# Small constants loaded behind a GpSimd read of a modulation chunk, and two modulation units transposed together

## The chip, the cores and the metric

The kernel runs on one core of a Trainium2 chip. A core has TensorE (PE in the profile, with its weight loads shown apart as PEld), VectorE (DVE), ScalarE (ACT), GpSimd (POOL) and SyncE (SP), each with an instruction stream of its own that runs in order. DMAs are issued by an engine's stream and carried out by the core's 16 DMA engines. The metric is the device time of one launch in microseconds, lower is better.

## The reference, cut to what matters

Two layers of a transformer trunk over 256 context tokens and 256 latent tokens, 1024 channels, in float32. Each layer begins so:

```python
mod_lat = (silu_c @ w_ada[l] + b_ada[l])[:, None, :]        # six shifts, scales, gates of 1024
mod_ctx = silu_ctx @ w_ada[l] + b_ada[l]
h_c = modulate(rms_norm(x_ctx, g_attn[l]), csh1, csc1)      # h * (1 + scale) + shift
h   = modulate(rms_norm(x_lat, g_attn[l]), sh1, sc1)
p = h @ w_in                                                # gates | c_q 768 | c_kv 256 | k_r 32 | q, k, v
mq = (rms_norm(c_q, g_qa) @ w_uq)
kv = (rms_norm(c_kv, g_kva) @ w_ukv)
mk = rms_norm(concat([k_nope, rope(k_r)]), g_mk)            # gains g_mla_q, g_mla_k, g_na_q, g_na_k
```

Two attentions follow (one dense, one over a window of a 4 x 64 grid with a learned position bias), a gated merge, an output projection and a squared-ReLU MLP. The small constants of this case are the gains `g_mla_q`, `g_mla_k`, `g_na_q`, `g_na_k`, the rope table, the window mask, a reversal matrix `rev`, and the second layer's biases and norm gains.

## The kernel before

Activations lie as [128 channels, 8 chunks, 512 tokens]. A product in float32 is made of three matmuls of float32r parts: `mm3` (L101 to L103) multiplies the high and low halves. A weight comes by `wraw` (L118, a DMA on SP's queue) into one of five `raw` buffers; `wsplit` makes `whi` on ACT (L127) and `wlo` on DVE (L128).

The opening of layer 0: `x` and the context are loaded and transposed, and the modulation of layer 0 that the first norm needs is computed in units. `ada_unit` (L183) loads two pieces of `w_ada` into `spare` buffers, multiplies them with `silu` on PE in float32 (L191), copies the sums on ACT (L197), transposes them on PE (L202), and finishes on DVE (L204, L208, and for a scale `A1` at L176). Groups of chunks `(0, 1), (1, 1), (2, 2), (4, 2), (6, 2)` (first chunk, how many) take a scale unit on PSUM bank C and a shift unit on bank D each (`ada2`, L474). `norm_apply` then makes `u` (L298, DVE, needs the scale), `h` high (L301, ACT, needs the shift) and `h` low (L303, DVE). The main product of that loop is c_q: per chunk 18 matmuls of 512 columns into six PSUM banks.

`late_consts` (L357) loads the constants with 16 DMAs on GpSimd's queue and then prepares them on DVE (L372 to L377). It is called behind the loop, with `tc.issue_after(r0_ins.ins)`, which lets its instructions be issued as soon as the reciprocal root of the first norm (L162) has been.

Behind that loop come, in this order of the program: the store of `xT` (L497), the evacuation of c_q (`lat_evac`, L508 to L512), the product for c_kv and k_r (`ckv_load`, `ckv_evac`, L595 to L619: copies `ckt` L600, squares L602 and L603 on ACT, `kr` L604, transposes L613, `G` at L617 and L618), a part of the modulation on DVE as side work (`ada_side`, L231 and L233, advanced by `step`), and the products with `w_uq` (three groups of heads, each of two loads) and `w_ukv`.

The engines' orders are not written by hand: a scheduler orders the instructions by the program's order, their dependencies and its own estimate of when each is ready. An edit in one place can therefore move instructions elsewhere. SP's order is the same in both kernels.

Of the kernel before, what the change touches and what calls it, by code (L numbers as in the profile page):

```python
# [7 lines left out]
F32 = mybir.dt.float32  # L8
F32R = mybir.dt.float32r
AF = mybir.ActivationFunctionType  # L10
ALU = mybir.AluOpType
AX = mybir.AxisListType.X

D = 1024
KD = 8
DEPTH = 2
# [6 lines left out]
NOPE = 64  # L23
# [22 lines left out]
def trunk(ctx: ExitStack, tc, t):  # L46
    nc = tc.nc
    PSUM = bass.MemoryType.PSUM
    const = ctx.enter_context(tc.tile_pool(name="const", bufs=1))
# [7 lines left out]
    def ps(tag):  # L57
        return pp.tile([128, 512], F32, tag="ps" + tag, name="ps" + tag, bufs=BANKS[tag])
# [19 lines left out]
    def bc(ap2d):  # L78
        return bass.AP(tensor=ap2d.tensor, offset=ap2d.offset, ap=[[0, 128]] + list(ap2d.ap))
# [36 lines left out]
    def wraw(w, k0, kc, c0, cols, alt=None):  # L116
        raw = v3(alt() if alt else raw_tile(), kc, cols)
        nc.sync.dma_start(  # L118
            out=raw,
            in_=w[k0 * 128:(k0 + kc) * 128, c0:c0 + cols].rearrange("(k p) f -> p k f", p=128),  # L120
        )
        return raw
# [27 lines left out]
    def step(n=1):  # L150
        while n and side:
            if next(side[0], side) is side:
                side.pop(0)
            else:
                n -= 1

    def rsqrt(dst, src):
        n = 1
        for d in src.shape[1:]:
            n *= d  # L160
        e = mhalf[:, 0:1].to_broadcast([128, n])
        return nc.gpsimd.tensor_tensor(out=dst, in0=src, in1=e, op=ALU.pow)  # L162
# [4 lines left out]
    A1 = [const.tile([128, KD, 2], F32, name=f"A1_{l}") for l in range(DEPTH)]  # L167
# [3 lines left out]
    def mod_use(l, j, f, n, m, zs=(0, 1)):  # L171

        if j in (1, 4):
            go = 48 if j == 1 else 56
            A = (A1 if j == 1 else A2)[l]
            nc.vector.scalar_tensor_tensor(  # L176
                out=A[:, f:f + n, zs[0]:zs[-1] + 1], in0=m, scalar=1.0,
                in1=pT[:, l, go + f:go + f + n].unsqueeze(2).to_broadcast([128, n, len(zs)]),
                op0=ALU.add, op1=ALU.mult)
        if j == 2:  # L180
            nc.vector.tensor_scalar(out=G1[l][:, f:f + n, zs[0]:zs[-1] + 1], in0=m, scalar1=0.5, scalar2=None, op0=ALU.mult)

    def ada_unit(l, j, f, bank="C", alt=None, defer=False, n=2):  # L183

        c0 = j * 8 + f
        o = ps(bank)
        for r in range(2):
            raw = wraw(t["w_ada"][l], r * 4, 4, c0 * 128, n * 128, alt)
            for g in range(4):
                k = r * 4 + g  # L190
                nc.tensor.matmul(  # L191
                    o[32 * g:32 * g + 32, :n * 128], silu[:, k], raw[:, g],
                    start=(r == 0), stop=(r == 1),
                    tile_position=(0, 32 * g),
                )
        s = sp.tile([128, 256], F32, tag="ada", name="ada", bufs=2)
        nc.scalar.activation(out=s[:, :n * 128], in_=o[:, :n * 128], func=AF.Copy)  # L197

        def second():
            o2 = ps(bank)  # L200
            for b in range(n):
                nc.tensor.transpose(o2[:, b * 128:(b + 1) * 128], s[:, b * 128:(b + 1) * 128], ident)  # L202
            m = modT[l][:, c0:c0 + n, :]
            nc.vector.tensor_reduce(  # L204
                out=m, in_=o2[:, :n * 128].rearrange("p (b g z) -> p b z g", b=n, g=4)[:, :, 0:2, :],
                op=ALU.add, axis=AX,
            )
            nc.vector.tensor_tensor(  # L208
                out=m, in0=m, in1=pT[:, l, c0:c0 + n].unsqueeze(2).to_broadcast([128, n, 2]), op=ALU.add)
            mod_use(l, j, f, n, m)  # L210

        if not defer:
            return second()
        ada_late.append(second)
# [60 lines left out]
    def r_bcast(r, T, bank="D"):  # L275
        o = ps(bank)
        for i in range(T // 128):
            nc.tensor.matmul(o[:, i * 128:(i + 1) * 128], r[:, i:i + 1].to_broadcast([128, 128]), ident,
                             start=True, stop=True)
        return o  # L280
# [30 lines left out]
    def load_rows(l, eng):  # L311
        o = 0
        for src, n in ((t["b_ada"][l], 48), (t["g_attn"][l], 8), (t["g_mlp"][l], 8), (t["g_qa"][l], 6),
                       (t["g_kva"][l], 2)):
            eng.dma_start(out=prow[l][o:o + n, :], in_=src.rearrange("(r q) -> r q", q=128))
            o += n
# [6 lines left out]
    warm = const.tile([128, 1], F32, name="warm")  # L323
# [3 lines left out]
    pre_ctx = ExitStack()  # L327
    xpool = pre_ctx.enter_context(tc.tile_pool(name="pre", bufs=1))
    xT = xpool.tile([128, KD, TT], F32, name="xT")
    gcm2 = xpool.tile([NOPE, DEPTH], F32, name="gcm2")  # L330
    gcn2 = xpool.tile([128, DEPTH], F32, name="gcn2")
    xrow = act.tile([128, 4096], F32, tag="G", name="xrow", bufs=2).rearrange("p (i d) -> p i d", i=4)
    for i in range(4):
        src = t["ctx"] if i < 2 else t["x"]
# [16 lines left out]
    def block_sum():  # L351
        id4 = ident.rearrange("p (q i) -> p i q", q=4)
        nc.vector.tensor_reduce(out=m32[:, 0:32], in_=id4, op=ALU.add, axis=AX)
        nc.vector.tensor_copy(m32[:, 32:128].rearrange("p (q i) -> p q i", q=3),
                              m32[:, 0:32].unsqueeze(1).to_broadcast([128, 3, 32]))

    def late_consts():  # L357
        dma = nc.gpsimd.dma_start
        dma(out=gqr, in_=bc(t["g_mla_q"][:, NOPE:QK]))
        dma(out=gkr, in_=bc(t["g_mla_k"][:, NOPE:QK]))  # L360
        dma(out=ropec, in_=t["rope"])
        dma(out=gcm[0:NOPE, :], in_=t["g_mla_q"][:, 0:NOPE].rearrange("l d -> d l"))
        dma(out=gcm2, in_=t["g_mla_k"][:, 0:NOPE].rearrange("l d -> d l"))
        for z in (0, HD):
            dma(out=gcn[z:z + HD, :], in_=t["g_na_q"].rearrange("l d -> d l"))
            dma(out=gcn2[z:z + HD, :], in_=t["g_na_k"].rearrange("l d -> d l"))
        dma(out=rev, in_=t["rev"])
        dma(out=wmask, in_=t["wmask"])
        load_rows(1, nc.gpsimd)

        keep, v = tc.keep_in_program_order, nc.vector
        keep(v.memset(gcm[NOPE:QK, :], 1.0))  # L372
        keep(v.tensor_scalar(out=gqr, in0=gqr, scalar1=QSC, scalar2=None, op0=ALU.mult))
        keep(v.scalar_tensor_tensor(out=gcm[0:NOPE], in0=gcm[0:NOPE], scalar=QSC, in1=gcm2, op0=ALU.mult, op1=ALU.mult))
        keep(v.scalar_tensor_tensor(out=gcn, in0=gcn, scalar=NSC, in1=gcn2, op0=ALU.mult, op1=ALU.mult))
        for l in range(DEPTH):
            keep(v.tensor_tensor(out=ropeq[:, l].rearrange("p a b d -> p (a b) d"),  # L377
                                 in0=ropec.rearrange("p a b d -> p (a b) d"),
                                 in1=gqr[:, l, :].unsqueeze(1).to_broadcast([128, 4, RD]), op=ALU.mult))
# [14 lines left out]
    ss0 = const.tile([128, 4], F32, name="ss0")  # L394
# [2 lines left out]
        nc.scalar.activation(out=junk, in_=xrow[:, i], func=AF.Square, accum_out=ss0[:, i:i + 1])  # L397
    nc.vector.tensor_scalar(out=ss0, in0=ss0, scalar1=1.0 / D, scalar2=EPS, op0=ALU.mult, op1=ALU.add)
    r0 = sp.tile([128, 4], F32, tag="rt", name="rt", bufs=4)
    r0_ins = rsqrt(r0, ss0)  # L400
    R0p = r_bcast(r0, TT, "A")
    R0 = sp.tile([128, TT], F32, tag="acc", name="R0", bufs=2)
    nc.vector.tensor_copy(R0, R0p)
# [45 lines left out]
    def flush():  # L449
        while ada_late:  # L450
            ada_late.pop(0)()

    for l in range(DEPTH):
# [20 lines left out]
        def ada2(gi):  # L474
            if l == 0 and gi < len(groups):
                k, n = groups[gi]
                ada_unit(0, 1, k, "C", alt, n=n)
                ada_unit(0, 0, k, "D", alt, n=n)

        ada2(0)  # L480
        for gi, (k0, n) in enumerate(groups):
            ks = range(k0, k0 + n)
# [9 lines left out]
        if l == 0:  # L492
            fill += [(1, j, f) for j in (4,3,5) for f in range(0, 8, 2)]
        if l == 0:
            with tc.issue_after(r0_ins.ins):
                late_consts()
        nc.sync.dma_start(out=xT_d, in_=xT)  # L497
        pre_ctx.close()
# [141 lines left out]
        if l == 0:  # L640
            block_sum()
            side.append(ada_side(((0, 2, (0, 1)),), lambda z: [ap.tile([128, TT], F32, tag="P", name="ada", bufs=4)
                                                               for _ in range(2)]))
            step(2)


        qrs, krr, krz = hstat("qrs"), hstat("krr"), hstat("krz")
# [274 lines left out]
        for f in range(0, 8, 2):  # L922
# [4 lines left out]
            for j in range(2):  # L927
# [9 lines left out]
                for b in range(2):  # L937
                    nc.vector.scalar_tensor_tensor(out=g2[:, b], in0=g2[:, b], scalar=1.0, in1=zs[b],
                                                   op0=ALU.add, op1=ALU.mult)
# [160 lines left out]
```

## Time and profile before

| | |
|---|---|
| three runs | 1344.7, 1344.02, 1344.84 us (median 1344.7) |
| the profiled execution | 1344.34 us |
| its span, first to last instruction | 1342.6 us |
| mean granted TensorE clock | 0.992 |
| bytes read from HBM, written | 195.15 MB, 11.53 MB |

In the profile, a row of the timeline gives start, duration, engine, line, operation, tiles written and read, shapes, count, and in brackets the idle time of the engine just before and what ended it. "DMA x" behind an arrow is the landing of that load. A row of the view by stages gives the stretch, its length, the busy time and number of instructions of PE, PEld, DVE, ACT and POOL, then the granted clock of PE, the mean busy share of the 16 DMA engines, and GB/s. A row of the waits gives who waited for whom, the sum in us, how often, and the longest. Rows of queues give packets, MB, and the share of the 16 engines' time; q0 is GpSimd's queue, q1 that of SP and ACT.

### The profile page before, as it was taken

The numbers are of one execution on the slowest core, as the hardware profiler recorded it, in microseconds if no ns is written. First come the engines' busy times: TensorE is split into PE (matmuls) and PEld (weight loads), VectorE is DVE, ScalarE is ACT, GpSimd is POOL, SyncE is SP. The second block draws the span as 40 slices with busy tenths as digits, with TensorE's granted clock in tenths as the row PEclk, the third lists the DMA queues.
The fourth block names the chain that finished last, engine by engine and source line by source line (L and its number), as shares of the span: only waits on it lengthen the run. The fifth ranks groups of instructions, "written<-read, shape, count | busy, mean of one in ns | idle before, by whom it ended". The sixth has DMA issues, their size and how long they took to land.

```text
span 1342.6 us, 20389 instructions
## 1 busy us (share of the span) xinstructions
PE 1306.7 (97%) x7825; PEld 1098.5 (82%) x7825; DVE 863.4 (64%) x1462; ACT 586.5 (44%) x1061; POOL 275.8 (21%) x296
## 2 busy tenths in 40 slices
PE   6999999999999989999999999998999999999997
PEld 4698888976687868888888888898889789899896
DVE  4589377867885588887574334765854766755453
ACT  3455366445423344331423313564654544554442
POOL 3035403401005003210201100056040121221111
PEclk8999999999999999999999999999999999999999
DMA  9865411544477645465473344575134769656652
GB/s 277 285 151 165 151 32 32 157 113 85 93 261 235 202 144 165 150 187 173 133 212 96 101 125 150 167 191 150 32 87 97 121 216 273 170 163 189 189 187 94
DMA packets 245985, 208.01 MB, mean 155 GB/s; under 512 B 24496, under 2 KB 226992, under 8 KB 245504
## 3 DMA queue, kind: packets, MB, share of 16 engines
q1 hardware_dynamic: 235856, 190.16, 49.9%
q10 hardware_dynamic: 9520, 16.29, 3.4%
q8 instruction: 61, 1.00, 0.3%
q0 software_dynamic: 512, 0.27, 0.2%
q14 instruction: 36, 0.29, 0.1%
HBM read 195.15 MB, written 11.53 MB: 154 GB/s over the span
## 4 chain that ended last, share of the span: by engine, by line
PE 57%; issue 5%; DMA 2%; DVE 1%; POOL 1%; ACT 1%; SPq 0%; POOLq 0%; ACTq 0%; DVEq 0%
PE psA L103 8%; PE psA L102 8%; PE psA L101 8%; PE psB L101 5%; PE psB L102 5%; PE psB L103 5%; PE psC L101 4%; PE psC L103 4%; PE psC L102 4%; DMA bias<-in_rpb_dram 1%; PE psD L833 1%; PE psC L806 1%; DMA raw<-in_w_ff_dram 1%; PE psD L101 1%; PE psD L102 1%
## 5 line engine op out<-in xcount | busy, mean ns | idle before, releaser
L128 DVE TENSOR_TENSOR wlo<-raw,whi 128x1024 fp32r<-128x1024 f32 (+3 forms) x254 | 311.8, 1229 | 209.2 <-ACT whi L127 203.4
L127 ACT ACTIVATE whi<-raw 128x1024 fp32r<-128x1024 f32 (+3 forms) x254 | 261.1, 1029 | 376.2 <-PE psA L102 110.1
L233 DVE SCALAR_TENSOR_TENSOR ada<-raw,silu,ada 128x1024 f32<-128x1024 f32 (+1 forms) x105 | 123.7, 1211 | 19.4 <-DMA raw<-in_w_ada_dram 19.3
L102 PE MATMUL psA<-wlo,h 128*128 128x256 f32 (+2 forms) x416 | 123.5, 297 | 0.5 <-DVE wlo L128 0.5
L101 PE MATMUL psA<-whi,h 128*128 128x256 f32 (+2 forms) x416 | 123.2, 296 | 0.0
L103 PE MATMUL psA<-whi,h 128*128 128x256 f32 (+2 forms) x416 | 122.8, 296 | 0.0
L102 PE MATMUL psA<-h,whi 128*128 128x512 f32 (+1 forms) x312 | 110.0, 354 | 0.0
L103 PE MATMUL psA<-h,wlo 128*128 128x512 f32 (+1 forms) x312 | 109.5, 353 | 0.0
L101 PE MATMUL psA<-h,whi 128*128 128x512 f32 (+1 forms) x312 | 109.0, 358 | 0.1
L101 PEld LDWEIGHTS psA<-whi,h 128*128 128x128 f32 x416 | 79.7, 192 | 2.9 <-issue 0.8
L102 PEld LDWEIGHTS psA<-wlo,h 128*128 128x128 f32 x416 | 79.7, 192 | 2.4 <-DVE wlo L128 0.8
L103 PEld LDWEIGHTS psA<-whi,h 128*128 128x128 f32 x416 | 79.7, 192 | 1.9 <-issue 0.4
L983 POOL TENSOR_TENSOR fl<-s,fa 128x512 fp32r<-128x512 f32 (+1 forms) x32 | 38.3, 1198 | 176.6 <-ACT fa L982 176.6
L103 PE MATMUL psB<-h,wlo 128*128 128x512 f32 (+1 forms) x208 | 72.5, 349 | 0.0
L102 PE MATMUL psB<-h,whi 128*128 128x512 f32 (+1 forms) x208 | 72.5, 349 | 0.0
L101 PE MATMUL psB<-h,whi 128*128 128x512 f32 (+1 forms) x208 | 72.2, 350 | 0.0
L983 POOL TENSOR_TENSOR h<-s,h 128x512 fp32r<-128x512 f32 (+1 forms) x32 | 36.9, 1153 | 169.2 <-ACT h L982 169.2
L101 PEld LDWEIGHTS psA<-h,whi 128*128 128x128 f32 x312 | 58.3, 190 | 12.6 <-issue 6.3
L103 PEld LDWEIGHTS psA<-h,wlo 128*128 128x128 f32 x312 | 59.4, 190 | 10.0 <-issue 3.1
L767 POOL TENSOR_TENSOR bias<-bias,wmask 128x512 f32<-128x512 f32 x16 | 21.7, 1355 | 223.2 <-DMA bias<-in_rpb_dram 183.9
L102 PEld LDWEIGHTS psA<-h,whi 128*128 128x128 f32 x312 | 59.4, 190 | 9.8 <-issue 2.9
L101 PE MATMUL psA<-G,whi 128*128 128x512 f32 (+1 forms) x184 | 65.1, 354 | 0.0
(353 smaller groups left out, 3363.9 us busy)
## 6 DMA issues: line engine op xcount, KB each, us to landing
raw<-in_w_ff_dram SPq DMA_DIRECT2D x128, 512.0 KB, 4.2
raw<-in_w_ada_dram SPq DMA_DIRECT2D x62, 512.0 KB, 4.2
raw<-in_w_in_dram SPq DMA_DIRECT2D x56, 512.0 KB, 4.1
spare<-in_w_ada_dram SPq DMA_DIRECT2D x30, 512.0 KB, 7.2
raw<-in_w_out_dram SPq DMA_DIRECT2D x16, 512.0 KB, 6.3
raw<-in_w_in_dram SPq DMA_DIRECT2D x16, 384.0 KB, 5.4
xT_d<-xT SPq DMA_DIRECT2D x2, 2048.0 KB, 11.8
bias<-in_rpb_dram SPq DMA_DIRECT2D x64, 64.0 KB, 7.1
```

The costliest lines, as they stand in the source:

```text
L101: nc.tensor.matmul(out, sh, mh, start=first, stop=False)
L102: nc.tensor.matmul(out, sh, ml, start=False, stop=False)
L103: nc.tensor.matmul(out, sl, mh, start=False, stop=last)
L127: nc.scalar.activation(out=hi, in_=src, func=AF.Copy)
L128: nc.vector.tensor_tensor(out=lo, in0=src, in1=hi.bitcast(F32), op=ALU.subtract)
L233: nc.vector.scalar_tensor_tensor(out=a, in0=raw[:, c:c + w], scalar=sc, in1=a, op0=ALU.mult, op1=ALU.add)
L767: nc.gpsimd.tensor_tensor(out=bias.rearrange("p a i j -> p (a i) j"), in0=bias.rearrange("p a i j -> p (a i) j"), in1=wmask.unsqueeze(1).t ...
L806: nc.tensor.transpose(o[:, kt * 256 + i * 128:kt * 256 + (i + 1) * 128], pt[:, (kp * 2 + kt) * 128:(kp * 2 + kt + 1) * 128], perm if K == ...
L833: return nc.tensor.matmul(yo[z * 64:(z + 1) * 64, oc], vsel(kt, 2 * hp + z), tr[kt // 2][:, kt % 2, :], start=kt == 0, stop=kt == nkt - 1, ...
L983: nc.gpsimd.tensor_tensor(out=al[:, f, :], in0=s[:, :TQ], in1=ah[:, f, :].bitcast(F32), op=ALU.subtract)
```

## The change

Four edits. The DMAs of `late_consts` are issued behind a new GpSimd instruction that reads `A1` of layer 0, chunk 5, and writes a scratch value. The DVE part of `late_consts` becomes `late_gains`, called later, after the first two steps of the side work. The two helper tiles `gcm2` and `gcn2` move to a pool that lives on. And `ada2` defers both units' second halves (transposes, reduction, sums) until both units' matmuls and copies are written.

```diff
-    gcm2 = xpool.tile([NOPE, DEPTH], F32, name="gcm2")
-    gcn2 = xpool.tile([128, DEPTH], F32, name="gcn2")
+    gcm2 = const.tile([NOPE, DEPTH], F32, name="gcm2")
+    gcn2 = const.tile([128, DEPTH], F32, name="gcn2")
...
         load_rows(1, nc.gpsimd)
 
+    def late_gains():
+
         keep, v = tc.keep_in_program_order, nc.vector
         keep(v.memset(gcm[NOPE:QK, :], 1.0))
...
-    r0_ins = rsqrt(r0, ss0)
+    rsqrt(r0, ss0)
...
-                ada_unit(0, 1, k, "C", alt, n=n)
-                ada_unit(0, 0, k, "D", alt, n=n)
+                ada_unit(0, 1, k, "C", alt, True, n)
+                ada_unit(0, 0, k, "D", alt, True, n)
+                flush()
...
-            with tc.issue_after(r0_ins.ins):
+
+            gate = nc.gpsimd.tensor_scalar(out=warm, in0=A1[0][:, 5, 0:1], scalar1=0.0, scalar2=0.0,
+                                           op0=ALU.mult, op1=ALU.add)
+            with tc.issue_after(gate.ins):
                 late_consts()
...
             step(2)
+
+        if l == 0:
+            late_gains()
```

The orders of the engines show where that puts things. On POOL, in the opening, the change's order has the gate (L499, `A_0_100` is `A1` of layer 0) ahead of the first constant:

```order
L162 TENSOR_TENSOR rt<-ss_187,mhalf 128x4
L499 TENSOR_SCALAR warm<-A_0_100 128x1
L359 DMA gqr<-in_g_mla_q_dram 128x2x32
L360 DMA gkr<-in_g_mla_k_dram 128x2x32
L361 DMA ropec<-in_rope_dram 128x128
```

Before, the DMA of `gqr` followed L162 directly; nothing else moved on POOL.

On DVE, in the c_kv stage, before the change (L233 is the side work of the modulation, L128 the split of a `w_uq` tile where it is 864 wide, `psA` the second pair of token blocks):

```order
L233 SCALAR_TENSOR_TENSOR ada<-raw,silu,ada 128x512 x3
L604 TENSOR_TENSOR kr<-psD,gkr 128x32
L618 SCALAR_TENSOR_TENSOR G<-psC,pT,G 128x256
L128 TENSOR_TENSOR wlo<-raw,whi 128x864
L233 SCALAR_TENSOR_TENSOR ada<-raw,silu,ada 128x512
L618 SCALAR_TENSOR_TENSOR G<-psC,pT,G 128x256
L600 COPY ckt<-psA 128x256
L270 TENSOR_SCALAR ms<-psD 128x4
L128 TENSOR_TENSOR wlo<-raw,whi 128x864
L600 COPY ckt<-psA 128x256
L233 SCALAR_TENSOR_TENSOR ada<-raw,silu,ada 128x512
L604 TENSOR_TENSOR kr<-psA,gkr 128x32 x2
```

and with it (L606, L610 and L624 are the L600, L604 and L618 of before):

```order
L233 SCALAR_TENSOR_TENSOR ada<-raw,silu,ada 128x512
L374 MEMSET gcm 32x2
L375 TENSOR_SCALAR gqr<-gqr 128x64
L376 SCALAR_TENSOR_TENSOR gcm<-gcm,gcm_114 64x2
L377 SCALAR_TENSOR_TENSOR gcn<-gcn,gcn_115 128x2
L379 TENSOR_TENSOR ropeq<-ropec,gqr 128x128 x2
L128 TENSOR_TENSOR wlo<-raw,whi 128x864
L606 COPY ckt<-psA 128x256
L270 TENSOR_SCALAR ms<-psD 128x4
L606 COPY ckt<-psA 128x256
L128 TENSOR_TENSOR wlo<-raw,whi 128x864
L610 TENSOR_TENSOR kr<-psA,gkr 128x32 x2
```

The L233 that opens the second piece is the fourth; the fifth, which stood between the two L618 before, now stands behind the two `kr`. The six preparations of the constants, which stood some 30 rows earlier, stand ahead of the first 864-wide `wlo`.

On ACT, in the same stage, before the change:

```order
L127 ACTIVATE whi<-raw 128x864
L617 ACTIVATE G<-psC,pT 128x256
L127 ACTIVATE whi<-raw 128x864
L602 ACTIVATE sq,kvss<-psA 128x256
L603 ACTIVATE sq,krs<-psA 128x32
L602 ACTIVATE sq,kvss<-psA 128x256
L603 ACTIVATE sq,krs<-psA 128x32
L617 ACTIVATE G<-psC,pT 128x256 x2
L671 ACTIVATE mqk<-psA 128x288
```

and with it (L608, L609, L623 and L680 are the L602, L603, L617 and L671 of before):

```order
L623 ACTIVATE G<-psC,pT 128x256
L127 ACTIVATE whi<-raw 128x864
L608 ACTIVATE sq,kvss<-psA 128x256
L609 ACTIVATE sq,krs<-psA 128x32
L608 ACTIVATE sq,kvss<-psA 128x256
L609 ACTIVATE sq,krs<-psA 128x32
L127 ACTIVATE whi<-raw 128x864
L623 ACTIVATE G<-psC,pT 128x256 x2
L680 ACTIVATE mqk<-psA 128x288
```

The last 864-wide `whi` of each piece is that of the third `w_uq` tile: it stood ahead of the squares of the second pair of token blocks, and now stands behind them.

## Prediction

> **What bounds the kernel now.** I read the page's engine table first, then its slices, then who waited for whom on PE.
>
> ```profile
> span 1342.6 us, 20389 instructions
> PE 1306.7 (97%) x7825; PEld 1098.5 (82%) x7825; DVE 863.4 (64%) x1462; ACT 586.5 (44%) x1061; POOL 275.8 (21%) x296
> PE   6999999999999989999999999998999999999997
> ...
> PE psC L735 <- POOL mqk L701: 3.5, 1, 3.5
> PE psD L191 <- DMA spare<-in_w_ada_dram: 2.4, 1, 2.4
> PE psC L613 <- DVE ckt L600: 1.1, 1, 1.1
> PE psA L101 <- DVE kr L604: 0.7, 1, 0.7
> ```
>
> TensorE is the bound: 1306.7 of 1342.6 us. Only the first of the 40 slices falls well below 9. So a change can win only where PE waits. Three of the waits quoted lie in the first 130 us, which is all the program that this change reorders: 2.4 us for a modulation weight, 1.1 us for the copy `ckt`, 0.7 us for `kr`. The profiled execution took 1344.34 us, 1.74 us more than its span. My sum is made against it. The median of the three runs, 1344.7, is 0.36 us higher.
>
> **Part 1: the constants leave the opening.** Stages first (PE, PEld, DVE, ACT, POOL busy, then granted clock, DMA share, GB/s), then the queues inside 16 to 20 us and inside 20 to 32 us.
>
> ```profile
> 12.00:16.00 4.00, 4.00 (x36) 2.80 (x34) 2.65 (x5) 2.42 (x6) 2.65 (x4) 1.00 1.15 318
> 16.00:20.00 4.00, 2.89 (x50) 1.46 (x49) 3.31 (x11) 1.80 (x5) 4.00 (x8) 1.00 0.84 103
> 20.00:27.00 7.00, 4.73 (x18) 3.45 (x19) 3.73 (x10) 2.70 (x6) 3.90 (x8) 0.51 1.08 328
> 40.00:56.00 16.00, 16.00 (x110) 10.23 (x103) 9.38 (x26) 6.36 (x14) 0.00 (x0) 1.00 0.97 357
> ...
> q0 software_dynamic: 78, 0.11, 54.3%
> q1 hardware_dynamic: 607, 0.30, 30.1%
> ...
> q0 software_dynamic: 434, 0.16, 6.4%
> ```
>
> DMA delivers 318 GB/s, then 103, then 328. In the bad 4 us, GpSimd's queue q0 holds the engines 54.3% of the time for 0.11 MB, and the weights' queue q1 gets 30.1%. Without q0 the weights gain 0.543 x 4 = 2.2 us of all engines, up to (318-103)/318 x 4 = 2.7 us by bytes. The later constants hold 6.4% of 12 us, 0.8 us.
>
> ```profile
> 19.76 0.91 ACT L301 ACTIVATE h<-u,modT 128x256 fp32r<-128x256 f32 x2 [0.62 <-DVE modT L208]
> 22.27 0.65 PE L191 MATMUL psD<-spare,silu 128*32 128x128 f32 x8 [2.39 <-DMA spare<-in_w_ada_dram]
> 22.86 1.22 PE L101 MATMUL psA<-h,whi 128*128 128x512 f32 x2
> ```
>
> PE stands 2.39 us before L191, and behind it in PE's order stand the first main matmuls, at 22.86. The weight would land 2.2 to 2.7 us earlier. The next thing late is `h` of chunk 0, ready at 19.76 + 0.91 = 20.67, unchanged. The first main matmul can therefore start near 20.7, about 2.1 us earlier. Bounds: 0, if this load is late for another reason, and -2.7. I take **-2.1**, the row of `h`.
>
> **Part 2: the constants arrive later.** Their gate reads `A1` of chunk 5, written at 41.83 + 0.16.
>
> ```profile
> raw<-in_w_in_dram SPq DMA_DIRECT2D x8, 384.0 KB, 7.7
> ...
> 40.79 0.93 SPq L118 DMA_DIRECT2D raw<-in_w_in_dram  x2
> 41.77 0.50 SPq L497 DMA_DIRECT2D xT_d<-xT  x1
> 41.83 0.16 DVE L176 SCALAR_TENSOR_TENSOR A<-modT,pT 128x4 f32<-128x4 f32 x1
> 52.90 0.64 PE L191 MATMUL psD<-spare,silu 128*32 128x256 f32 x8
> 53.94 0.84 ACT L127 ACTIVATE whi<-raw 128x768 fp32r<-128x768 f32 x1
> 14.33 0.93 POOL L359 DMA_DIRECT2D gqr<-in_g_mla_q_dram  x1
> 26.15 0.51 POOL L315 DMA_DIRECT2D prow<-in_g_kva_dram  x1
> 77.11 0.18 DVE L604 TENSOR_TENSOR kr<-psC,gkr 128x32 f32<-128x32 f32 x1
> ```
>
> All 16 issues took 26.15 + 0.51 - 14.33 = 12.3 us, so they run from 42 to 55. Behind the gate on POOL stand only these DMAs, and then the bias additions after 76 us. The first reader is `kr` at 77.11, 22 us after the last issue. The burst now meets the load of chunks 6 and 7 (issued 40.79, used at 53.94) and the 2 MB store of `xT`, which PE does not wait for. It takes at most 2.7 us from the weights, and 53.94 - 41.72 is 12.2 us, against the 7.7 us that such loads of 384 KB take to land in the opening (median, first row). Cost 0. With that cover gone it would be 2.7.
>
> The Trainium skill, "DMA: Bandwidth & Descriptors", section "Issuing engines are not separate DMA queues", speaks against the change: DMAs of all issuing engines share the same 16 DMA engines and interleave. The rows of q0 and q1 agree (54.3% beside 30.1%). By that rule the burst costs its 2.2 us wherever it lands while DMA is full (0.97 in 40 to 56 us), and the sum would be 2.1 us worse; by the rows it takes the time from the store.
>
> **Part 3: the units' transposes together.** The counts of matmuls, copies and reductions are the same. Only the order changes: the scale unit's transposes now stand on PE behind the shift unit's matmuls, so `A1` comes later by a block of eight L191 at most, 0.64 us (row 52.90). What hides it: `h` needs the shift unit too, and its wait at 19.76 was ended by that unit's `modT` (L208), not by `A1`. If it were not hidden it would cost up to 0.6 once, since only the first group stands ahead of an idle PE; grouping the transposes could as well spare PE a change between kinds of matmul, of which no row gives a price by itself, so I bound the gain by the same block. Bounds -0.6 to +0.6, taken as 0.
>
> **Part 4: the late gains and what the scheduler moved with them.** This decides more than the diff suggests.
>
> ```profile
> 79.91 0.47 DVE L618 SCALAR_TENSOR_TENSOR G<-psC,pT,G 128x256 fp32r<-128x256 f32 x1
> 58.58 0.06 DVE L372 MEMSET gcm<- 32x2 f32 x1
> 58.92 0.48 DVE L377 TENSOR_TENSOR ropeq<-ropec,gqr 128x128 f32<-128x128 f32 x2
> 83.40 0.75 DVE L233 SCALAR_TENSOR_TENSOR ada<-raw,silu,ada 128x512 f32<-128x512 f32 x1 [2.05 <-DMA raw<-in_w_ada_dram]
> 84.94 0.45 PE L613 MATMUL psC<-ident,ckt 128*128 128x128 f32 x1 [1.15 <-DVE ckt L600]
> 87.50 0.93 ACT L127 ACTIVATE whi<-raw 128x864 fp32r<-128x864 f32 x1 [5.91 <-DMA raw<-in_w_uq_dram]
> 89.33 0.37 PE L101 MATMUL psA<-whi,G 128*128 128x288 f32 x1 [0.73 <-DVE kr L604]
> 82.00:85.00 3.00, 1.85 (x15) 1.62 (x15) 1.60 (x5) 0.00 (x0) 0.00 (x0) 1.00 0.79 194
> 85.00:88.40 3.40, 3.30 (x13) 2.85 (x13) 1.91 (x3) 0.90 (x2) 1.87 (x2) 0.50 0.78 250
> 88.40:89.30 0.90, 0.21 (x2) 0.00 (x0) 0.19 (x1) 0.90 (x9) 0.65 (x1) 0.99 0.38 155
> ```
>
> The six DVE instructions take 58.92 + 0.48 - 58.58 = 0.8 us. They leave an idle place and now stand ahead of `wlo`. But the fifth L233, which waited 2.05 us for its DMA ahead of both `ckt` copies, now stands behind them, and so does ACT's L127 of the third `w_uq` tile, which waited 5.91 us ahead of the squares that `kr` needs. Both PE waits lose their cause. PE lost 1.15 idle, 1.65 at half clock (half of 3.30) and 0.69, together 3.5 us; the later `wlo` gives back some 0.4, leaving 3.1.
>
> What is late next?
>
> ```profile
> 95.12 2.02 DVE L128 TENSOR_TENSOR wlo<-raw,whi 128x864 fp32r<-128x864 f32 x2
> 96.82 0.29 PE L102 MATMUL psA<-wlo,G 128*128 128x288 f32 x1
> 89.30:96.70 7.40, 7.37 (x56) 7.40 (x57) 7.16 (x13) 3.97 (x11) 6.96 (x11) 1.00 0.29 74
> 96.70:118.00 21.30, 21.30 (x163) 20.60 (x161) 20.02 (x34) 12.17 (x25) 6.25 (x9) 1.00 0.77 230
> ```
>
> The third `w_uq` tile. Its ACT split still waits for the same DMA, near 87.5, and the order puts the same twelve L233 ahead of its `wlo` as before, plus the 0.8 us of gains, which fall into the time in which DVE waited before. I put that `wlo` at 95.1 again: ready at 96.1, and PE used it at 96.82. DVE is busy 7.16 of 7.40 us there, so there is little to catch up with. PE's gain of 3.1 shrinks to 96.82 - 96.1 = **-0.7**, and PE stands idle some 2.4 us ahead of 96 instead. The row 85.00:88.40 shows what followed such a gap: 3.4 us at half clock, 1.7 us of work. Before, it lay partly beside waits; after 96.7 PE is busy without a gap. Bounds 0 and 1.7; I take **+1.2**, since DVE, 20.02 of 21.30 busy, hides part.
>
> Sum: -2.1 - 0.7 + 1.2 = -1.6 us. 1344.34 - 1.6 = **1342.7 us**, all else carried through, since PE is never long without work afterwards.
>
> **Rivals.**
> *Both gains stay* (0.22): the third tile's `wlo` comes 2.4 us earlier, because the two DVE waits vanish and their time is not refilled, and no clock is lost. 1344.34 - 2.1 - 3.1 = 1339.1. For it: DVE waited 2.05 us at 83.40. Against: 87.50, the same DMA.
> *The wait moves and grows* (0.10), the slower one: the third `w_uq` load needs the buffer that the eighth modulation product (the fourth L233) frees, and ahead of it now stand two L618 at 0.47 and one L604 at 0.18. It lands 1.1 us later, the gains' 0.8 us are not hidden, and the clock stays half for as long as from 20 to 27 us, 3.4 us lost: -2.1 + 1.9 + 3.4 = +3.2, 1347.5. With half as long a spell 1345.8. It decides from a `wlo` that starts more than 2.1 us later than 95.1, counted from the first main matmul, as the opening's gain is then used up. For it: 0.50 in the row of 85.00. Against: the load's landing at 87.5 was set by a DMA stage at 0.78, not by its issue.
> *The opening's gain fails or is paid back at 42 to 55 us* (0.13): -1.6 + 2.1, 1344.8; that the gate did not hold the loads back is in it, though POOL's order puts it first.
>
> The Trainium skill, "TensorE: Matmul & The Clock Gate", Part 1, says the clock is judged in free-running windows of about 3.4 us and is full again after one busy window. The 3.40 us row agrees, the 7 us one only as two windows. By the rule, the opening's half clock could end one window earlier and the sum would be about 0.6 us better.
>
> **How the numbers follow.** Forecast 0.55, with its own range 1341.2 to 1344.2. A measurement of this kernel tells about 0.2%, 2.7 us, from no change: 1342.0 to 1347.4 counts as same. Faster: the first rival and a fifth of the forecast, 0.33. Slower: half of the second rival, 0.05. Same 0.62. The range 1339.6 to 1346.2 leaves out half of the first rival and half of the second.
>
> **What would show it.** Right: GB/s in 16 to 20 us near 320; first L101 near 20.7; no wait of PE for `ckt` or `kr` before 95; a wait for `wlo` ahead of the second w_uq group. Wrong: the L191 wait still above 1 us; PE waiting between 40 and 56 us; no gap before that `wlo`, which would be the first rival.

## The result, and the profile after

The changed kernel takes **1338.96 us** (median of six runs, 1335.59 to 1340.72), the kernel before 1344.77 (six runs, 1341.44 to 1346.71). The ratio is 0.9948, with a 95% interval of 0.9931 to 0.9965: 5.8 us or 0.5% faster. The forecast was 1342.7, with a range down to 1339.6; the rival "both gains stay" had 1339.1. The profiled execution took 1338.82 us. A run far outside the others (3249.89 us in one of transposes_only, 1590.79 and 5351.93 in two of the kernel before) counts in no ratio below.

The page of the changed kernel, its engines and the slices of PE:

```profile
span 1337.0 us, 20381 instructions
PE 1305.0 (98%) x7825; PEld 1097.4 (82%) x7825; DVE 862.5 (65%) x1462; ACT 587.3 (44%) x1061; POOL 278.9 (21%) x297
PE   7999999999999989999999999998999999999997
```

PE's busy time fell by 1.7 us and the span by 5.6: most of what went is idle time. The same shows in who waited for whom on PE from 14 to 130 us:

```profile
PE psA L102 <- DVE wlo L128: 1.1, 1, 1.1
PE psA L101 <- ACT h L301: 0.8, 1, 0.8
```

The waits for L191's weight (2.4), for `ckt` (1.1) and for `kr` (0.7) are gone. Two new ones stand first: 0.8 us for `h`, and 1.1 us for a `wlo`. The stages (PE, PEld, DVE, ACT, POOL, then granted clock, DMA share, GB/s):

```profile
16.00:20.00 4.00, 3.31 (x55) 2.08 (x57) 3.23 (x9) 1.46 (x4) 0.00 (x0) 1.00 0.77 210
20.00:27.00 7.00, 6.22 (x35) 4.69 (x27) 4.29 (x14) 2.81 (x6) 0.00 (x0) 0.76 1.05 343
40.00:56.00 16.00, 16.00 (x100) 10.82 (x99) 10.80 (x26) 7.51 (x15) 9.51 (x16) 1.00 1.00 358
82.00:85.00 3.00, 3.00 (x25) 3.00 (x24) 1.12 (x4) 1.29 (x2) 2.61 (x2) 1.00 0.85 283
85.00:88.40 3.40, 3.40 (x27) 3.24 (x26) 3.40 (x7) 2.27 (x6) 3.23 (x7) 1.00 0.07 27
89.30:96.70 7.40, 6.25 (x47) 6.02 (x47) 7.40 (x12) 2.73 (x6) 3.64 (x6) 1.00 0.61 202
```

In 16 to 20 us DMA moves 210 GB/s where it moved 103. The granted clock of the opening is 0.76 over 20 to 27 us where it was 0.51. From 40 to 56 us the constants are loaded (16 instructions on POOL) and PE is busy 16.00 of 16.00. From 82 to 88.4 us PE is full at full clock, where it stood, and then ran at half clock, before.

To measure stages across kernels I use two marks. The c_kv stage begins about where DVE first evacuates c_q (L512 of the kernel before), and the first modulation's side work ends at L255. DVE's timeline, before:

```profile
66.56 0.75 DVE L512 SCALAR_TENSOR_TENSOR G<-psA,pT,G 128x512 fp32r<-128x512 f32 x1
127.27 0.72 DVE L255 TENSOR_TENSOR modT<-psC,pT 32x16 f32<-32x16 f32 x4
```

and after, where L512 has become L518, with the split of the third `w_uq` tile between them (the first of the two in that row):

```profile
63.91 0.75 DVE L518 SCALAR_TENSOR_TENSOR G<-psA,pT,G 128x512 fp32r<-128x512 f32 x1
90.80 2.03 DVE L128 TENSOR_TENSOR wlo<-raw,whi 128x864 fp32r<-128x864 f32 x2
122.45 0.72 DVE L255 TENSOR_TENSOR modT<-psC,pT 32x16 f32<-32x16 f32 x4
```

The opening is 66.56 - 63.91 = **2.65 us** shorter, and the stage between the marks lasts 58.54 us where it lasted 60.71, **2.17 us** less. The view by stages over just that stretch, before and after:

```profile
66.56:127.27 60.71, 58.47 (x394) 54.79 (x393) 54.19 (x98) 33.17 (x76) 25.91 (x38) 0.97 0.64 162
63.91:122.45 58.54, 57.15 (x394) 53.62 (x393) 54.48 (x105) 33.72 (x76) 27.03 (x38) 1.00 0.64 168
```

PE has the same 394 matmuls and is idle for 2.24 us before and 1.39 after. The clock is 0.97 before: one spell of 3.4 us at half clock (85.00 to 88.40), 1.7 us of work. After, there is none. From the second mark to the end the two profiles differ by another 0.8 us, which the last section explains.

### The profile page after: what moved, and what is told of

Same layout as the page of the kernel before. It is cut to its first block, busy times and chain, and to the rows that moved or that the text cites. A ratio compares the mean times of both kernels' runs of the same rounds, so it can differ in the third digit from the quotient of the medians.

```text
span 1337.0 us, 20381 instructions
## 1 busy us (share of the span) xinstructions
PE 1305.0 (98%) x7825; PEld 1097.4 (82%) x7825; DVE 862.5 (65%) x1462; ACT 587.3 (44%) x1061; POOL 278.9 (21%) x297
## 4 chain that ended last, share of the span: by engine, by line
PE 57%; issue 5%; DMA 2%; DVE 2%; ACT 2%; POOL 1%; SPq 0%; POOLq 0%; ACTq 0%; DVEq 0%
PE psA L101 8%; PE psA L103 8%; PE psA L102 8%; PE psB L101 5%; PE psB L102 5%; PE psB L103 5%; PE psC L101 4%; PE psC L102 4%; PE psC L103 4%; DMA bias<-in_rpb_dram 1%; PE psC L815 1%; DVE wlo L128 1%; PE psD L842 1%; PE psD L101 1%; PE psD L103 1%
## 5 line engine op out<-in xcount | busy, mean ns | idle before, releaser
L128 DVE TENSOR_TENSOR wlo<-raw,whi 128x1024 fp32r<-128x1024 f32 (+3 forms) x254 | 311.6, 1229 | 210.8 <-ACT whi L127 203.8
L233 DVE SCALAR_TENSOR_TENSOR ada<-raw,silu,ada 128x1024 f32<-128x1024 f32 (+1 forms) x105 | 121.9, 1196 | 18.2 <-DMA raw<-in_w_ada_dram 18.1
L101 PE MATMUL psA<-G,whi 128*128 128x512 f32 (+1 forms) x184 | 65.4, 355 | 0.0
L102 PE MATMUL psA<-G,whi 128*128 128x512 f32 (+1 forms) x184 | 65.3, 355 | 0.0
```

The lines of the kernel that those rows point to most:

```text
L101: nc.tensor.matmul(out, sh, mh, start=first, stop=False)
L102: nc.tensor.matmul(out, sh, ml, start=False, stop=False)
L128: nc.vector.tensor_tensor(out=lo, in0=src, in1=hi.bitcast(F32), op=ALU.subtract)
L233: nc.vector.scalar_tensor_tensor(out=a, in0=raw[:, c:c + w], scalar=sc, in1=a, op0=ALU.mult, op1=ALU.add)
```

## The experiments

All runs first, with the two marks of their profiles; after_again, after_third and gate_transposes_again repeat a kernel. A ratio is to the runs of the kernel before in the same job. "Order" says where ACT's split `whi` of the third `w_uq` tile stands: ahead of the squares of the last c_kv tokens, as before, or behind them, as after. "Opening" is the start of the row of L512, "stage" the time from there to L255.

| kernel | gate | transposes | gains | order | opening | stage | median (runs) | ratio to before, 95% |
|---|---|---|---|---|---|---|---|---|
| before | no | apart | old | ahead | 66.56 | 60.71 | 1344.77 (6) | |
| after | yes | together | late | behind | 63.91 | 58.54 | 1338.96 (6) | 0.9948 [0.9931, 0.9965] |
| after_again | yes | together | late | behind | 61.62 | 57.85 | 1338.39 (7) | 0.9962 [0.9945, 0.9979] |
| after_third | yes | together | late | behind | 62.34 | 58.06 | 1338.08 (7) | 0.9964 [0.9947, 0.9982] |
| gate_only | yes | apart | old | ahead | 64.31 | 60.37 | 1342.26 (10) | 0.9984 [0.9966, 1.0002] |
| transposes_only | no | together | old | behind | 65.88 | 58.10 | 1340.9 (7) | 0.9962 [0.994, 0.9983] |
| gains_only | no | apart | late | ahead | 66.98 | 62.09 | 1344.15 (10) | 1.0001 [0.9986, 1.0017] |
| gate_gains | yes | apart | late | ahead | 63.36 | 59.75 | 1340.94 (6) | 0.9965 [0.995, 0.998] |
| gate_transposes | yes | together | old | behind | 63.85 | 56.90 | 1336.69 (4) | 0.9938 [0.9915, 0.996] |
| gate_transposes_again | yes | together | old | behind | 62.79 | 57.17 | 1337.19 (8) | 0.9954 [0.9936, 0.9972] |
| act_order_only | no | apart | old | behind, forced | 64.96 | 58.64 | 1342.44 (10) | 0.9996 [0.9982, 1.0011] |
| gate_act_order | yes | apart | old | behind, forced | 62.81 | 58.20 | 1338.6 (10) | 0.9964 [0.995, 0.9979] |
| broadcasts_late | two loads | apart | old | ahead | 63.78 | 58.66 | 1341.28 (10) | 0.9983 [0.9967, 0.9999] |
| broadcasts_early | the other 14 | apart | old | ahead | 65.74 | 60.75 | 1342.2 (10) | 0.9991 [0.9977, 1.0004] |

### The parts apart, and in pairs

Four kernels undo parts of the change. gate_only keeps the gate alone, transposes_only is the kernel before with the edit of `ada2` alone, gate_transposes and gate_gains leave out one part each. Against the changed kernel, gate_only and gate_transposes call the gains at their old place:

```diff
             with tc.issue_after(gate.ins):
                 late_consts()
+            late_gains()
...
-        if l == 0:
-            late_gains()
```

and gate_only and gate_gains transpose each unit by itself again:

```diff
-                ada_unit(0, 1, k, "C", alt, True, n)
-                ada_unit(0, 0, k, "D", alt, True, n)
-                flush()
+                ada_unit(0, 1, k, "C", alt, n=n)
+                ada_unit(0, 0, k, "D", alt, n=n)
```

> Only the gate: the constants' 16 DMAs wait for the scale of chunk 5; gains prepared at their old place, units transposed one by one. Every engine's order is that of before but for the gate. Theory A (two separate gains: the gate frees the opening, the transposes' edit frees the c_kv stage): first main matmul near 21.2 us instead of 22.9, everything at 70 us 2.7 us earlier, and still 2.7 us earlier (not 4.8) at 127 us; the waits of PE for ckt (about 1.1) and kr (about 0.7) stay. Theory B (the third w_uq load lands earlier because the constants have left, and this frees the c_kv stage): 4.8 us earlier at 127 us, the waits for ckt and kr gone. Time: A 1342, B 1340.

> Only the two units of a group transposed together. Theory A: L191's wait for its weight stays at 2 to 2.4 us and nothing is earlier at 70 us (0, within 0.3), but at 127 us all is 2.2 us earlier, and PE waits neither for ckt nor for kr. Theory B: 0 at 70 us and 0 at 127 us. Time: A 1342.5, B 1344.8.

> Gate and transposes, gains prepared at their old place on DVE. Theory A: 2.7 us earlier at 70 us and 4.8 to 5.6 us earlier at 127 us, since the 0.8 us of gains no longer stand ahead of wlo. If the late place of the gains is what opened the c_kv stage (theory C): 2.7 us at both. Time: A 1339.5, C 1342.

> Gate and late gains, units transposed one by one. Theory A: 2.7 us earlier at 70 us, and at 127 us the same or up to 0.8 us less, since the gains stand on DVE ahead of the first 864-wide wlo and the waits for ckt and kr stay. Theory C (the late gains opened the c_kv stage): 4.8 us at 127 us. Time: A 1342.5, C 1340.

The two gains separate. PE's waits from 14 to 130 us with the gate alone:

```profile
PE psA L101 <- DVE kr L610: 2.0, 1, 2.0
PE psA L101 <- ACT h L301: 0.6, 1, 0.6
```

and with the transposes alone:

```profile
PE psD L191 <- DMA spare<-in_w_ada_dram: 1.6, 1, 1.6
PE psA L102 <- DVE wlo L128: 1.1, 1, 1.1
```

The gate removes L191's wait and leaves that for `kr` (the one for `ckt` is gone too, which theory A had staying); the transposes' edit removes `ckt` and `kr` and leaves L191's. By time alone the gate is not clear of noise (0.9984 [0.9966, 1.0002]); the mark at L512 is what shows it. The theory that the earlier landing of the weights frees the c_kv stage falls: in gate_only the third `w_uq` tile was split at 83.34 us, 4.2 us earlier than before, and PE still waited 2.0 us for `kr`. The theory that the late gains opened that stage falls too, since gate_gains has them and its stage is 59.75 us against 56.90 in gate_transposes, which doesn't.

### Only the order on ACT

transposes_only moved more than transposes: the order of ACT in the c_kv stage came out as in the changed kernel, and so did DVE's up to the last `kr`, but for the gains. So the next two kernels add nothing but an ordering edge from ACT's split to the last square, once on gate_only and once on the kernel before. The transposes stay apart, and SP's order is the same. DVE's order did not stay: the scheduler put the second `ckt` copy ahead of the 864-wide `wlo` and `kr` ahead of the L233 that had stood before it, so the two kernels show ACT's order together with that.

```diff
-            nc.scalar.activation(out=sq[:, KVL:KVL + RD], in_=o[:, KVL:], func=AF.Square, accum_out=krs[:, tk:tk + 1])
+            last_sq[0] = nc.scalar.activation(out=sq[:, KVL:KVL + RD], in_=o[:, KVL:], func=AF.Square, accum_out=krs[:, tk:tk + 1])
...
+            def load_behind(i):
+                with tc.issue_after(last_sq[0].ins):
+                    return load(i)
+
-            proj_b(load, 2, lambda k: ch[:, k], lambda k: cl[:, k],
+            proj_b(load_behind if l == 0 and h0 == 3 else load, 2, lambda k: ch[:, k], lambda k: cl[:, k],
```

> The gate alone (as gate_only) and one thing more: on ScalarE the split (whi) of the third w_uq tile is held behind the squares of the last c_kv tokens, by an ordering edge and nothing else; the transposes of the units stay apart, the gains stay at the old place. Theory A2 (what the transposes' edit brought in the c_kv stage is only this order on ScalarE): PE's wait for kr, 2.0 us in gate_only, goes; the third w_uq split still starts near 83 us, where its DMA lands; at 120 to 130 us everything stands 6.5 us earlier than in the profile of before (gate_transposes 6.5, gate_only 2.6); median 1336.5 to 1339.5. Rival B2 (the order of the transposes on PE, or the modulation loads' own order, is what pays): kr's wait goes but a wait of the same 2 us comes in its place, and 120 to 130 us stays at 2.6 to 3.5 us earlier; median 1340.5 to 1343.

> The kernel of before with the ScalarE ordering edge alone: no gate, no transposes' change, no late gains. Theory A2: opening as before (L191 waits about 2 us for its DMA), 0 at 70 us; PE's waits for ckt and kr go, 120 to 130 us stands 2.6 to 3.3 us earlier; median 1340.5 to 1342.5. Rival B2: 120 to 130 us within 1 us of before, since the third w_uq split waits for the same DMA near 87.5 us and a wait for wlo of 2 us or more takes their place; median 1343 to 1345.

ACT's timeline in gate_only shows what the edge removes:

```profile
83.34 0.92 ACT L127 ACTIVATE whi<-raw 128x864 fp32r<-128x864 f32 x1 [4.01 <-DMA raw<-in_w_uq_dram]
84.17 0.37 ACT L608 ACTIVATE sq<-psA 128x256 f32<-128x256 f32 x1
84.53 0.19 ACT L609 ACTIVATE sq<-psA 128x32 f32<-128x32 f32 x1
```

and in gate_act_order what it makes of it:

```profile
79.86 0.39 ACT L609 ACTIVATE sq<-psA 128x256 f32<-128x256 f32 x1 [2.02 <-DVE ms L270]
80.75 0.20 ACT L610 ACTIVATE sq<-psA 128x32 f32<-128x32 f32 x1
82.17 0.93 ACT L127 ACTIVATE whi<-raw 128x864 fp32r<-128x864 f32 x1 [0.75 <-DMA raw<-in_w_uq_dram]
```

In the first, ACT stands 4.01 us before a split whose load is not there, with the squares behind it, and `kr` behind them. In the second the squares go first, and the split waits 0.75 us with nothing held up behind it. The stage fell from 60.37 to 58.20 us with the gate, and from 60.71 to 58.64 without it: 2.1 to 2.2 us, as in the changed kernel (2.2 to 2.9 in its three profiles). The stage's rows of gate_only, gate_act_order and act_order_only say of what this is made:

```profile
64.31:124.68 60.37, 58.09 (x394) 55.02 (x393) 54.84 (x99) 33.19 (x76) 25.81 (x38) 0.97 0.63 163
62.81:121.01 58.20, 56.58 (x394) 53.48 (x393) 54.79 (x98) 33.16 (x76) 28.16 (x42) 1.00 0.65 169
64.96:123.60 58.64, 57.08 (x394) 53.49 (x393) 54.05 (x98) 33.28 (x76) 28.61 (x38) 1.00 0.65 168
```

PE's idle time fell by only 0.7 us, from 2.28 to 1.62 and from 2.24 to 1.56. The rest is a spell of 3.4 us at half clock, 1.7 us of work, that is gone. Four of the six profiles with the old order have such a spell in this stage, none of the eight with the new order. The two with the old order and no spell, gate_gains and broadcasts_late, stand at 59.75 and 58.66 us. So the order removes the wait for `kr`, and the spell behind it did not come in any profile with the new order; the transposes themselves are not needed for it. How much it is worth in one execution hangs on whether the spell would have come: 2.1 to 2.2 us with it, and by the difference to its 1.7 us 0.4 to 0.5 without.

The times point the same way with the gate (0.9964 [0.995, 0.9979] against 0.9984 [0.9966, 1.0002] in gate_only), but the intervals overlap. Without it act_order_only was 3.67 us ahead at L255, of which 1.6 us stood at L512 already, and 1.9 us at the end of its profile; the last section shows where the rest went. Its ratio, 0.9996 [0.9982, 1.0011], shows no gain, so over the whole run the order alone is not shown to pay; the stage is what shows it.

A wait for `wlo` of 1.4 us (gate_act_order) and 1.0 us (act_order_only) took the place of the others. In the two profiles of gate_transposes it was nothing and 0.3. Why the stage is 1.1 us shorter with the transposes together than with the edge stays open; only one profile of gate_act_order stands against two.

### The late gains, and the same kernels again

gains_only moves the six preparations alone (with their two helper tiles), on the kernel before. after_again and after_third repeat the changed kernel, and gate_transposes_again stands beside the latter in one job.

```diff
+    def late_gains():
+
         keep, v = tc.keep_in_program_order, nc.vector
...
             step(2)
+
+        if l == 0:
+            late_gains()
```

> The kernel of before with only the six VectorE gains moved behind the first two steps of the sixth modulation. Theory A: 0 at 70 us, since their old place was idle; 0 to 0.8 us later at 120 to 130 us, since VectorE is full there; median 1343.5 to 1345.5. Rival C (the gains at their late place change what VectorE does in the c_kv stage for the better): 1.5 us or more earlier at 120 to 130 us.

> The changed kernel unchanged, profiled a second time. Theory A: the same waits: none for L191, ckt or kr, 1.0 to 1.2 us for wlo of the third w_uq tile, 120 to 130 us stands 4.5 to 5.1 us earlier than before's profile; the half-clock windows after 200 us stand at other places, and the end moves by up to 2.5 us for them. Rival (the wait for wlo hangs on where the third w_uq load happens to land, not on the order): the wait comes out under 0.5 or over 1.7 us, with a landing that moves by as much.

> The changed kernel with the gains back at their old place, a second time, for its interval and beside the changed kernel. Theory F (the late gains cost up to 1.7 us in the c_kv stage, as the first profiles had it): from 70 to 127 us it gains 3.3 to 4 us on before, against 2.2 and 2.9 in the two profiles of the changed kernel; median 1336 to 1337.7, at least 1 us under the changed kernel's in the same job. Rival G (the gains' place changes nothing, the first profile was a lucky one): 2.2 to 2.9 us from 70 to 127 us, median 1338 to 1339.5, within 0.7 us of the changed kernel's.

> The changed kernel once more, in the same job as gate_transposes_again and over as many rounds. Theory F: median 1338 to 1339.5, PE waits 0.5 to 1.2 us for wlo of the third w_uq tile. Rival G: the same median, within 0.7 us of gate_transposes_again.

gains_only kept PE's wait for `kr`:

```profile
PE psA L101 <- DVE kr L606: 3.6, 1, 3.6
PE psD L191 <- DMA spare<-in_w_ada_dram: 1.4, 1, 1.4
```

and its stage was 62.09 us, 1.4 us longer than before, where theory A had 0 to 0.8. With the gate alone the late gains seem to shorten the stage (59.75 us in gate_gains, 60.37 in gate_only), but gate_only has a half-clock spell there and gate_gains has not; without the spell's 1.7 us gate_gains is 1.1 us longer. With gate and transposes the late gains lengthen the stage from 56.90 and 57.17 us to 58.54, 57.85 and 58.06: the means are 57.04 and 58.15, 1.1 us apart, and no profile of one lies among those of the other. None of these five has a half-clock spell in the stage. So the gains did cost about 1.1 us there, as theory F had it, though less than its 1.7. The times point the same way, 1337.19 against 1338.08 us in one job, but by 0.9 us where theory F asked for 1, and their intervals overlap (0.9954 [0.9936, 0.9972] and 0.9964 [0.9947, 0.9982]). **gate_transposes**, the change without the late gains, beats the kernel before, and is not shown to beat the changed one.

The repeated profiles of the changed kernel put the wait for `wlo` at 0.5 us in both, against 1.1 in the first. That part of theory A missed, and the rival that it hangs on where the load lands is half right: the split of that tile started at 80.34 and 81.29 us there, at 83.31 in the first.

### Which of the constants hold the opening

`late_consts` has 16 loads. Two, `gqr` and `gkr`, spread one row over all 128 partitions. The last pair of kernels gates these two alone, or the other fourteen alone. broadcasts_late against gate_only (broadcasts_early has the two calls exchanged):

```diff
+    def late_rows():
+        dma = nc.gpsimd.dma_start
         dma(out=gqr, in_=bc(t["g_mla_q"][:, NOPE:QK]))
         dma(out=gkr, in_=bc(t["g_mla_k"][:, NOPE:QK]))
...
+            with tc.issue_after(r0_ins.ins):
+                late_consts()
...
             with tc.issue_after(gate.ins):
-                late_consts()
+                late_rows()
```

> The gate holds back only the two loads that spread one row over all 128 partitions (gqr, gkr; 32 KB each); the other fourteen loads of constants go out in the opening, as before the change. Theory D (those two loads are what holds the DMA engines in 16 to 20 us: q0 took 54.3% of the engines there for 0.11 MB): the opening is as with the whole gate: first main matmul 21.0 to 21.5 us, DMA near 200 GB/s in 16 to 20 us, no wait of L191 over 0.5 us, 65 to 75 us stands 2.3 to 3.7 us earlier than in before's profile; median as gate_only, 1341 to 1343. Rival E (the many small packets of the others, 544 packets under 512 B, or their number, do it as much): L191 still waits over 0.9 us, GB/s under 130 in 16 to 20 us, 65 to 75 us at 0 to 1.6 us earlier; median 1343 to 1345.

> The other half of the same split: only gqr and gkr go out in the opening, the other fourteen loads are held by the gate. Theory D: the opening is as before the change: L191 waits 0.9 to 2.4 us for its DMA, first main matmul 21.9 to 22.9 us, GB/s in 16 to 20 us at 80 to 130, 65 to 75 us within 1.6 us of before's profile; median 1343 to 1345. Rival E: first main matmul near 21.3, 65 to 75 us 2.3 us earlier or more; median 1341 to 1343.

The queues in 16 to 20 us of broadcasts_early:

```profile
q0 software_dynamic: 55, 0.07, 47.7%
q1 hardware_dynamic: 659, 0.33, 34.8%
```

and of broadcasts_late:

```profile
q1 hardware_dynamic: 1063, 0.76, 70.8%
q0 software_dynamic: 128, 0.07, 7.3%
```

Here the two loads alone hold the engines 47.7% of the 4 us and leave the weights 0.33 MB; the other fourteen hold 7.3%, and the weights get 0.76 MB. PE waited 2.3 us for L191's weight in broadcasts_early (opening 65.74 us, among the ungated), and its first main matmul came at 20.70 us in broadcasts_late (opening 63.78, among the gated). Theory D holds for this wait. It missed in one thing: broadcasts_late has another wait of L191, 1.1 us on bank C, so the fourteen are not free. The times don't separate the two: broadcasts_early's 1342.2 us lies outside theory D's 1343 to 1345, and the intervals overlap.

## Why the prediction was wrong

**Part 1, the opening, -2.1: right in sign, mis-sized.** Over the eight profiles with the whole gate the opening ends at 61.62 to 64.31 us (mean 63.12), over the four without any of it at 64.96 to 66.98 (mean 66.10): -3.0 us, of which about 1.1 is PE's idle time and about 1.9 work at half clock. The cause was the one named. `h` is what is late next, 0.8 us of wait, and the first main matmul starts at 21.23 us, not 20.7, since `h` itself came 0.52 us later than in the first profile:

```profile
20.28 0.91 ACT L301 ACTIVATE h<-u,modT 128x256 fp32r<-128x256 f32 x2 [0.78 <-DVE modT L208]
```

Over all the profiles of this case that row starts between 19.58 and 20.56 us, with either order of the transposes, so I had taken one early start for the rule. The start gave only 1.63 us. What the term had left out is the clock: 20 to 27 us ran at 0.51 before and at 0.76 after, and at 1.00 in five of the eight gated profiles. Weighed by PE's busy time this is 4.73 x 0.49 - 6.22 x 0.24 = 0.8 us in the two first profiles, and 2.3 us where the clock stays full.

The sign I had given for it, GB/s near 320 in 16 to 20 us, failed: 210. DMA's share is 0.77 there, so without the constants the engines are not what holds the weights; their buffers are. SP, which issues them, waited between 12 and 22 us for matmuls that free a buffer, 3.1 us before and in the changed kernel:

```profile
SPq L118 <- PE psD L191: 3.6, 1, 3.6
```

**Part 2, the constants at 40 to 56 us, 0: right, and for one reason more than I gave.** q0 takes little of the engines in that stretch:

```profile
q1 hardware_dynamic: 2508, 5.43, 93.2%
q0 software_dynamic: 508, 0.27, 5.9%
```

and PE is busy all of it. 5.9% of 16 us is 0.9 us of all engines; the rows of the opening had 2.2 + 0.8 for the same loads. So there was less to hide than I thought. The Trainium skill, "DMA: Bandwidth & Descriptors", section "Issuing engines are not separate DMA queues", says that DMAs run on the same 16 DMA engines whichever engine starts them. The rows agree, but the price of 2.1 us that I had worked out by it did not come.

**Part 3, the transposes together, 0: wrong in what it covered.** No direct price shows above the spread of the openings, as said. But the edit also changed the order of ACT and DVE 40 us later, and the stage there became 2.6 us shorter without the gate, and 3.2 to 3.5 with it, the half-clock spell included. I had seen the new order and counted it under Part 4, as something that the late gains brought. gains_only shows that they don't.

**Part 4, -0.7 + 1.2: this is the step that failed.** "I put that `wlo` at 95.1 again" and "Its ACT split still waits for the same DMA, near 87.5" did not hold. The split started at 83.31 us:

```profile
83.31 0.93 ACT L127 ACTIVATE whi<-raw 128x864 fp32r<-128x864 f32 x1 [1.49 <-DMA raw<-in_w_uq_dram]
```

and the `wlo` at 90.80 us in the first profile, 87.81 and 88.76 in the others. For the stage the two terms make +0.5 us; it measured -2.17. Two things were missed. I shifted PE by the opening's 2.1 us but left the landing where it was, though the load is issued by the same stage: the split, which waited for its load in every profile, started at 80.34 to 83.34 us in the eight with the whole gate and at 85.52 to 87.72 in the four without, and gate_only alone has 83.34. That is more than the opening's shift: counted from the mark at L512 the split came 18.7 to 19.8 us later in the eight and 20.0 to 20.9 in the four, and why stays open. And I let DVE's queue stay full, "busy 7.16 of 7.40", though its waits of 2.05 us (L233, for its load) and 2.09 + 0.35 us (`kr`, for the squares) stood just ahead and were gone with the new order; one new wait of 1.88 us came (the `G` of L624, for ACT). With as many L233 ahead of it the `wlo` could come that much earlier. The half clock that I added for the gap before it did not come in any of the three profiles. PE's wait there is this one:

```profile
91.90 0.40 PE L102 MATMUL psA<-wlo,G 128*128 128x288 f32 x1 [1.15 <-DVE wlo L128]
```

What did hold of Part 4: the waits for `ckt` and `kr` went, and the late gains take DVE's time ahead of that `wlo`. They were priced at nothing and cost about 1.1 us.

**The rivals.** "Both gains stay", 1339.1, was the case, for the reason it gave: DVE's two waits vanish, are refilled only by the 1.88 us, and no clock is lost. I had given it 0.22, and the row of 87.50 as evidence against it. That its time came so close is in part luck: it had -2.1 and -3.1, and the profiles have -2.65, -2.17 and another 0.8 us far behind the stage. "The wait moves and grows" did not come: the load was issued later against the shifted stage, as it said, and landed earlier all the same.

## What to carry to other kernels

When an in-order engine stands waiting for a load with ready work behind it, that work can be put first by one ordering edge; here this took 0.7 us off PE's idle time in the stage, and a half-clock spell of 1.7 us of work went with it. When a wait goes, shift everything that hung on it, landings and queues of other engines too, before naming what is late next. An edit that reorders one place should be compared on every engine's order over the whole program, and a shift at one mark, in several profiles and with the half clock counted apart, tells parts apart that the total time does not.

## What the runs showed of the hardware

**The same few packets can hold the DMA engines in one place and cost little in another.** In 16 to 20 us of the kernel before, q0's 78 packets took 54.3% of 16 engines over 4 us, 0.45 us each, while q1's 607 took 0.03 us each; per byte that is about five times as long. The split shows that most of it belongs to the two loads of 32 KB that spread a row over the partitions. But these loads are not slow by themselves. In 44 to 48 us of broadcasts_late they are all that q0 moves:

```profile
q1 hardware_dynamic: 364, 1.71, 107.6%
q0 software_dynamic: 64, 0.07, 4.9%
```

There they take 4.9% of the engines, where they took 47.7% in broadcasts_early. The packets beside them on q1 hold 4.7 KB on average (1.71 MB in 364), and held 0.5 KB in the opening (0.33 MB in 659). Whether that, or something else of the opening, makes them slow no run separates.

**Half clock after short gaps, at places that change from run to run.** The stretch from 484 to 496 us is the same program in all kernels. In the kernel before:

```profile
484.00:488.00 4.00, 3.46 (x32) 1.91 (x28) 2.83 (x9) 0.77 (x2) 1.50 (x1) 1.00 0.68 226
488.00:492.00 4.00, 2.96 (x28) 1.79 (x28) 2.05 (x8) 0.78 (x2) 0.49 (x1) 1.00 0.21 35
492.00:496.00 4.00, 3.03 (x12) 2.28 (x13) 4.00 (x13) 2.26 (x5) 0.00 (x0) 1.00 1.00 336
```

in the changed kernel:

```profile
488.00:492.00 4.00, 3.59 (x9) 2.65 (x10) 4.00 (x12) 2.38 (x5) 0.00 (x0) 0.62 0.93 312
```

and in act_order_only:

```profile
484.00:488.00 4.00, 3.04 (x20) 2.18 (x18) 2.33 (x5) 0.38 (x1) 1.54 (x1) 0.69 0.22 67
492.00:496.00 4.00, 4.00 (x12) 2.95 (x11) 4.00 (x12) 2.56 (x6) 0.00 (x0) 0.57 0.73 246
```

PE's waits there, in the kernel before:

```profile
PE psB L101 <- ACT G L301: 1.3, 1, 1.3
PE psC L191 <- issue: 1.1, 1, 1.1
PE psD L278 <- POOL rt L162: 1.0, 1, 1.0
```

They are the same to 0.2 us in the three kernels, and yet between 484 and 496 us the clock halves nowhere, once, or twice. Of its three profiles the changed kernel has the spell here in two. act_order_only has three spells under work behind L255, these two and one at 1048 us; the kernel before has two, at 931 and 1146 us. One spell more, 1.7 us of work, is nearly all of the 1.8 us that act_order_only lost there. The spell at 1146 us:

```profile
1144.00:1148.00 4.00, 3.44 (x25) 1.86 (x26) 1.66 (x5) 1.16 (x4) 0.71 (x1) 0.82 0.95 270
```

The changed one has none there, but the one at 489 us, so the two cancel. The last 0.8 us between the two profiles is a wait: PE stood 2.41 us for ACT's copy (L202 behind L197) at 1144.56 us before, and 1.62 at 1140.61 in the changed kernel. The Trainium skill, "TensorE: Matmul & The Clock Gate", Part 1, calls the window of about 3.4 us free-running. That agrees: in the kernel before the spells start at 20.1, 85.0, 931.5 and 1146.5 us, to 0.1 us whole multiples of 3.413 us apart, so the same gaps fall differently into the windows of each execution. The Trainium skill, "TensorE: Matmul & The Clock Gate", section "Why this matters for your kernels", advises to keep idle gaps between bursts of matmuls under some 3 us. That is too wide here: three gaps of 1.0 to 1.3 us were enough in two of the three kernels.

This is also the spread of the times. Over the ten runs of gate_only the slowest took 1346.42 us at a mean granted clock of 0.991 and the fastest 1337.56 at 0.998: 0.7% of clock beside 0.66% of time. A profile or two per kernel can therefore be misled by 2 us at the end. The marks at 64 and 125 us are reached before most of these spells, though the stretches from 20 to 28 and from 85 to 93 us have some of them.
